# First norm and first four FFN tiles made block by block of rows, with the loads in that order

## The chip, the cores and the metric

The kernel runs on one core of a Trainium2 chip. The metric is device microseconds of one execution. Line numbers (L194) are those of the kernel file; in the changed kernel every helper stands one line lower (L195 for L194).

## The reference

The reference is two layers of a transformer block on 512 rows (256 of context, 256 of latent), each layer: a gated FFN half step, four parallel token mixers, another FFN half step. Only its first step matters here:

```python
def ada_mods(cond, w, b):
    m = jax.nn.silu(cond) @ w + b
    m = m.reshape(m.shape[:-1] + (N_MOD, D_MODEL))
    return [m[..., i, :][..., None, :] for i in range(N_MOD)]

def swiglu_half_step(x, g, shift, scale, gate, w1, w3, w2):
    h = modulate(rms_norm(x, g), shift, scale)      # h * (1 + scale) + shift
    return x + MACARON_W * gate * ((jax.nn.silu(h @ w1) * (h @ w3)) @ w2)
```

D_MODEL is 1024, D_FF is 2816 (22 tiles of 128), N_MOD is 9. The first half step needs modulations 0 (shift) and 1 (scale), one set for the context (`c_ctx`) and one for the latent rows (`c`).

## The kernel before

Data lie with features on the 128 partitions, in 8 blocks of 128 (`k`), and the 512 rows along the free axis: `X[128, 8, 512]`. Every large product is made in three matmuls per block, from a rounded high part and a residue of both operands (`hi`, `lo` of a weight, `hh`, `hl` of the normed rows): hi·hh, hi·hl, lo·hh. A weight tile (128 x 1024, 512 KB) is loaded to `wr` (3 buffers) by SyncE's queue (SP) and split in two halves (`parts`, `split`): ScalarE rounds the high part (`wh`, or `aa` and `ar` for the first tile), VectorE or POOL subtracts for the low part (`wl`). `LSEQ` and `EARLY` say which of the two does it, "V" or "P"; `EARLY[0]` is "PVPV".

The start of the program, up to the steady run of the first FFN, is what the change touches:

- `run` (L1863 and after) loads parameters, X in two halves, constants and a mask (`lvm`), makes the sums of squares (`sq_acc`), and runs `ada0`: 16 loads of 512 KB (two modulations, 8 blocks of the contraction), and for each block 4 matmuls of 512 columns with only 32 columns of weights (the conditions `cs`), all summed in one PSUM bank. `ada_finish` copies the result and transposes it. So the modulations of all 1024 features come out together, after the last load. After two of the 16 loads `rstd_a` sums the squares over the partitions (matmuls with one column) and takes the reciprocal root on VectorE.
- `norm` gives the normed rows in two column halves (rows 0 to 255, 256 to 511): `rstd_b` spreads the root over the partitions, then each block takes a product with x and the gain (VectorE, `nt`), a rounding with the shift added (ScalarE, `hh`) and a residue (VectorE, `hl`).
- `ffn` splits the weights of tiles f = 0 and 1 (w1 and w3 each: four products, which I call the first four FFN tiles), and `heads` makes the four products over the first half of the columns, then over the second. Then the loop over f takes w1 and w3 of a tile over all 512 columns, 24 matmuls each, with the activation behind, and steps the background work `ada` (the other modulations, on VectorE: scale and add, 128 x 1024) in between.

Matmuls of one engine run in the order in which a scheduler has put them when the kernel is built; `issue_after` and `high_priority` steer it, and a tile name with few buffers makes a later writer wait for its readers.

Of the kernel before, what the change touches and what calls it, by code (L numbers as in the profile page):

```python
# [8 lines left out]
F32 = mybir.dt.float32  # L9
# [4 lines left out]
ALU = mybir.AluOpType  # L14
# [11 lines left out]
def bc(ap, axis, n):  # L26
    a = ap.unsqueeze(axis)
    shp = list(a.shape)
    shp[axis] = n
    return a.broadcast_to(shp)  # L30


def constants():
# [93 lines left out]
class Ker:  # L127
# [1205 lines left out]
    def gemm(s, ps, hi, lo, xh, xl, n, first, last, m=128, mid=None):  # L1333

        for k in range(n):
            if k == n // 2 and mid:
                sec = s.sec
                mid()
                s.sec = sec
            st, sp = first and k == 0, last and k == n - 1  # L1340
            s.mm(ps, hi[k][:, 0:m], xh(k), start=st, stop=False)
            s.mm(ps, hi[k][:, 0:m], xl(k), start=False, stop=False)
            s.mm(ps, lo[k][:, 0:m], xh(k), start=False, stop=sp)
# [20 lines left out]
    def ada0(s, pool):  # L1364

        raws = {}
        cs = s.t(pool, "cs", [128, 8, 32])
        s.nc.gpsimd.memset(cs, 0.0)
        s.nc.vector.tensor_copy(cs[:, :, 0:2], s.cs)
        ps = s.psum("o")  # L1370
        for n in range(KC + 4):
            if n < KC:
                raws[n] = [s.ada_fetch(0, i, n, pool, 12) for i in range(2)]
            if n >= 4:
                kc = n - 4
                s.sec = "ada0"
                for j in range(4):
                    s.mm(ps[32 * j:32 * j + 32], cs[:, kc], raws[kc][j // 2][:, 512 * (j % 2):512 * (j % 2) + 512], start=(kc == 0), stop=(kc == KC - 1))
                yield
        v = s.ada_finish(0, 0, 2, ps)  # L1380
        ov = s.mod[0][:, 0:16].rearrange("p (j q) t -> p j q t", q=4)
        bv = s.p["adab"][:, 0, 0:16].rearrange("p (j q) -> p j q", q=4)
        s.tt(ov, v[:, :, :, 0:2], bc(bv, 3, 2), ALU.add)

    def ada(s, todo):

# [179 lines left out]
    def ffn(s, l, j, lat, bga, bgb, nxt):  # L1566

        nc = s.nc
        a = 256 if lat else 0
        hh, hl, part, todo = s.nh  # L1570
        gate = s.t(s.xp, "gate", [128, 8, 2], bufs=2)
        with s.tc.tile_pool(name=s.nm("fp"), bufs=1) as fp:
            gh, gl = (s.moved(fp, z, FF, 16) for z in ("gh", "gl"))
            with s.tc.tile_pool(name=s.nm("fa"), bufs=1) as fa:
                s.ar = (fa, 3, 2, hl[:, 7, 511:512].bitcast(F32))
                s.bg = [s.ada(bga)]
                def early(i, dram):
# [3 lines left out]
                ws = [early(i, s.I[n][l, j, 0]) for i, n in enumerate(("w1", "w3"))]  # L1581
                with s.tc.issue_after(s.lastq.ins) if lat else nullcontext():
                    ws += [s.piece(s.I[n][l, j, 1]) for n in ("w1", "w3")]
                hs4 = [s.psum("gm"[i % 2]) for i in range(4)]
                s.lseq = LSEQ["ffa"]
                s.heads(ws, hs4, (hh, hl), lat, todo or part(256 if lat else 0, 512 if lat else 256), part)
# [276 lines left out]
    def run(s, out):  # L1863
# [9 lines left out]
        with s.tc.tile_pool(name="st", bufs=1) as st:  # L1873
            for k in range(0, 8, 4):
                nc.sync.dma_start(s.X[:, k:k + 4], s.I["xT"][:, k:k + 4])
            nc.sync.dma_start(s.cst[:, 0:129], s.I["cst"][:, 0:129])
            lv = s.t(st, "lv", [128, 384])
            nc.sync.dma_start(lv, s.I["lvm"])
            nc.gpsimd.tensor_copy(s.mk.rearrange("p a b -> p (a b)"), lv)
            s.tt(s.i64, s.ident[:, 0:64], s.ident[:, 64:128], ALU.add, nc.gpsimd)  # L1880
            s.sec = "x"
            for d in range(7):
                s.sq_acc(d, 0, 512)
            for sp in s.parts2(False):
                s.sq_acc(7, *sp)
            s.bg = [s.ada0(st)]
            s.step(2)
            s.early = {sp[0]: s.rstd_a(*sp) for sp in s.parts2(False)}
            s.step(1000)
        s.late = [(s.cst[:, 129:], s.I["cst"][:, 129:CST_OFF["cos"][0]])]  # L1890
        nil = lambda p: []
        s.nh = *s.norm(0, 0), None
# [77 lines left out]
def pack_weights(inp):  # L1970
# [50 lines left out]
```

## Time and profile before

| | us |
|---|---|
| median of 3 runs (2442.76 to 2445.41) | 2444.49 |
| the profiled execution | 2443.27 |
| its span, first to last instruction | 2441.5 |
| TensorE busy | 2351.9 (96%) |
| VectorE busy | 1717.7 (70%) |
| ScalarE busy | 977.9 (40%) |
| POOL busy | 164.9 (7%) |
| read from HBM | 311.45 MB |

The profiled execution took 2443.27 us, of which 1.8 lie around its span. Busy shares are means over a program of many stages; what a change in the first 64 us is worth is read from those 64 us. In the profile an fp32 matmul stands as two records, and a matmul's duration is longer than its distance to the next one, because matmuls are pipelined. "x24" merges 24 instructions of a kind.

### The profile page before, as it was taken

The numbers are of one execution on the slowest core, as the hardware profiler recorded it, in microseconds if no ns is written. First come the engines' busy times: TensorE is split into PE (matmuls) and PEld (weight loads), VectorE is DVE, ScalarE is ACT, GpSimd is POOL, SyncE is SP. The second block draws the span as 40 slices with busy tenths as digits, with TensorE's granted clock in tenths as the row PEclk, the third lists the DMA queues.
The fourth block names the chain that finished last, engine by engine and source line by source line (L and its number), as shares of the span: only waits on it lengthen the run. The fifth ranks groups of instructions, "written<-read, shape, count | busy, mean of one in ns | idle before, by whom it ended". The sixth has DMA issues, their size and how long they took to land.

```text
span 2441.5 us, 41204 instructions
## 1 busy us (share of the span) xinstructions
PE 2351.9 (96%) x15690; PEld 1957.5 (80%) x15690; DVE 1717.7 (70%) x4146; ACT 977.9 (40%) x1900; POOL 164.9 (7%) x167
## 2 busy tenths in 40 slices
PE   7999999999999999999999999999999989898998
PEld 4887788867778788888788887878887868788998
DVE  4888797667865676688886787853367876786555
ACT  4333323344454443433332333332233654455554
POOL 1111100000000000011110011110000000000110
PEclk9999999999999999999999999999999999899999
DMA  6656444421212122366634455643343312234554
GB/s 266 206 198 212 151 138 156 152 84 57 78 61 70 53 79 70 131 205 207 207 96 134 142 174 189 208 138 93 98 132 116 105 57 92 80 120 158 184 181 136
DMA packets 116902, 330.34 MB, mean 135 GB/s; under 512 B 11872, under 2 KB 38624, under 8 KB 116320
## 3 DMA queue, kind: packets, MB, share of 16 engines
q1 hardware_dynamic: 116704, 327.71, 41.2%
q8 instruction: 123, 2.02, 0.3%
q14 instruction: 75, 0.61, 0.1%
HBM read 311.45 MB, written 16.22 MB: 134 GB/s over the span
## 4 chain that ended last, share of the span: by engine, by line
PE 85%; DVE 8%; ACT 3%; DMA 2%; issue 2%; POOL 0%; SPq 0%; DVEq 0%; ACTq 0%; POOLq 0%
PE ffa__g L194 17%; PE ffa__m L194 17%; PE ffb__g L194 15%; PE mrg__g L194 9%; PE win__g L194 8%; PE dn__m L194 3%; PE mrg__p L194 2%; PE out__g L194 2%; PE s__m L194 2%; PE hg__m L194 1%; PE at__m L194 1%; DMA s5ab<-tab__s5o 1%; DVE dn__it L212 1%; DVE dn__iw L212 1%; DMA ada__ar<-in_ada 1%
## 5 line engine op out<-in xcount | busy, mean ns | idle before, releaser
L209 ACT ACTIVATE ffa__wh<-ffa__wr 128x512 fp32r<-128x512 f32 x336 | 211.3, 631 | 421.5 <-PE ffa__m L194 151.4
L215 DVE SCALAR_TENSOR_TENSOR ada__aa<-ada__ar,x__cs,ada__aa 128x1024 f32<-128x1024 f32 x224 | 314.2, 1428 | 18.0 <-DMA ada__ar<-in_ada 17.4
L212 DVE TENSOR_TENSOR ffa__wl<-ffa__wr,ffa__wh 128x512 fp32r<-128x512 f32 x334 | 231.8, 702 | 125.4 <-ACT ffa__wh L209 124.2
L194 PE MATMUL ffa__g<-nrm__hh,ffa__wh 128*128 128x512 f32 (+1 forms) x696 | 250.1, 359 | 0.0
L194 PE MATMUL ffa__g<-nrm__hh,ffa__wl 128*128 128x512 f32 (+1 forms) x696 | 249.3, 358 | 0.0
L194 PE MATMUL ffa__g<-nrm__hl,ffa__wh 128*128 128x512 f32 (+1 forms) x696 | 248.6, 357 | 0.0
L194 PE MATMUL ffa__m<-nrm__hh,ffa__wh 128*128 128x512 f32 (+1 forms) x696 | 248.5, 357 | 0.0
L194 PE MATMUL ffa__m<-nrm__hl,ffa__wh 128*128 128x512 f32 (+1 forms) x696 | 248.3, 357 | 0.0
L194 PE MATMUL ffa__m<-nrm__hh,ffa__wl 128*128 128x512 f32 (+1 forms) x696 | 247.9, 356 | 0.0
L212 DVE TENSOR_TENSOR ffb__wl<-ffb__wr,ffb__wh 128x512 fp32r<-128x512 f32 x192 | 123.8, 647 | 144.2 <-ACT ffb__wh L209 143.2
L209 ACT ACTIVATE ffb__wh<-ffb__wr 128x512 fp32r<-128x512 f32 x192 | 113.9, 595 | 238.8 <-PE ffb__g L194 190.1
L194 PE MATMUL mrg__g<-nrm__hh,mrg__wh 128*128 128x256 f32 (+1 forms) x440 | 153.2, 348 | 3.8 <-ACT mrg__wh L209 1.9
L194 PEld LDWEIGHTS ffa__g<-nrm__hh,ffa__wh 128*128 128x128 f32 x696 | 132.3, 190 | 27.2 <-ACT ffa__wh L209 9.2
L194 PE MATMUL mrg__g<-nrm__hh,mrg__wl 128*128 128x256 f32 (+1 forms) x440 | 149.6, 340 | 2.9 <-DVE mrg__wl L212 2.9
L194 PEld LDWEIGHTS ffa__m<-nrm__hh,ffa__wh 128*128 128x128 f32 x696 | 131.7, 189 | 22.0 <-ACT ffa__wh L209 3.4
L194 PE MATMUL mrg__g<-nrm__hl,mrg__wh 128*128 128x256 f32 (+1 forms) x440 | 148.9, 338 | 0.0
L194 PEld LDWEIGHTS ffa__g<-nrm__hh,ffa__wl 128*128 128x128 f32 x696 | 132.0, 190 | 18.5
L194 PEld LDWEIGHTS ffa__g<-nrm__hl,ffa__wh 128*128 128x128 f32 x696 | 132.1, 190 | 18.3
L194 PEld LDWEIGHTS ffa__m<-nrm__hh,ffa__wl 128*128 128x128 f32 x696 | 131.6, 189 | 18.6
L194 PEld LDWEIGHTS ffa__m<-nrm__hl,ffa__wh 128*128 128x128 f32 x696 | 131.6, 189 | 18.4
L209 ACT ACTIVATE mrg__wh<-mrg__wr 128x512 fp32r<-128x512 f32 x128 | 79.6, 630 | 140.7 <-PE mrg__g L194 63.3
L194 PE MATMUL ffb__g<-nrm__gh,ffb__wh 128*128 128x256 f32 (+1 forms) x374 | 123.5, 330 | 0.0
(637 smaller groups left out, 5568.7 us busy)
## 6 DMA issues: line engine op xcount, KB each, us to landing
ffa__wr<-in_w SPq DMA_DIRECT2D x176, 512.0 KB, 3.9
ada__ar<-in_ada SPq DMA_DIRECT2D x144, 512.0 KB, 4.1
ffb__wr<-in_w SPq DMA_DIRECT2D x64, 512.0 KB, 3.5
mrg__wr<-in_wgt SPq DMA_DIRECT2D x64, 512.0 KB, 3.5
win__wr<-in_win SPq DMA_DIRECT2D x48, 512.0 KB, 3.6
ffb__wr<-in_w SPq DMA_DIRECT2D x32, 384.0 KB, 3.1
mrg__wr<-in_wbr SPq DMA_DIRECT2D x16, 512.0 KB, 3.5
out__wr<-in_wout SPq DMA_DIRECT2D x16, 512.0 KB, 3.9
```

The source lines that it names most:

```text
L194: s.last = s.nc.tensor.matmul(out=out, lhsT=lhsT, rhs=rhs, start=start, stop=stop, skip_group_check=True)
L209: s.lasta = s.nc.scalar.activation(out=out, in_=in_, func=f, **kw)
L212: (eng or s.nc.vector).tensor_tensor(out=out, in0=a, in1=b, op=op)
L215: s.nc.vector.scalar_tensor_tensor(out=out, in0=a, scalar=sc, in1=b, op0=op0, op1=op1)
```

## The change

`start0` takes the place of `ada0`, of the first `norm` and of the first `heads`. The weights of the first two modulations are packed anew (`in_ada0`): one piece of 1 MB for each block of 128 output features, holding the whole contraction for its shift and its scale. For each block there are 8 matmuls of 256 columns (`products`; contraction blocks 0 to 3 and 4 to 7 land in four column groups of the array), a copy by ScalarE, and two matmuls with the two columns of a new constant `sel4`, which add the four groups and turn the result (`block`; I call them the selection). Then the block's modulation, gain, product, rounding and residue follow for all 512 rows, and `gemm` gives this block's three matmuls of 512 columns to each of the four tiles, tiles 2 and 3 two blocks behind tiles 0 and 1. Loads are issued in the order of use. All low parts of the weights are made by VectorE. The mask's load goes behind all this, into a buffer of the norm. The raw pieces lie in the room of `gh` and `gl`, which are taken again afterwards. The background modulations and everything behind the first four tiles stay.

```diff
-EARLY = ("PVPV", "VVVV", "VVVV", "VVVV")
+EARLY = ("VVVV", "VVVV", "VVVV", "VVVV")
...
+    c["sel4"] = p[:, None] % 32 == np.arange(2)[None]
...
+    def start0(s, fp, early, ps4):
...
+        nc.sync.dma_start(s.X[:, 0:4], s.I["xT"][:, 0:4])
+        fetch(0)
+        nc.sync.dma_start(s.X[:, 4:8], s.I["xT"][:, 4:8])
...
+        for k in (1, 2):
+            fetch(k)
...
+        def products(k):
+            s.sec = "ada0"
+            ps = s.psum("p")
+            for kc in range(8):
+                j = kc % 4
+                s.mm(ps[32 * j:32 * j + 32, 0:256], cs[:, kc], raw[k][:, kc], start=(kc < 4), stop=(kc >= 4))
+            ev = room[0][:, 8192 + 256 * (k % 4):8448 + 256 * (k % 4)]
+            s.act(ev, ps[:, 0:256], AF.Copy)
+            return ev
+
+        def block(k, ev):
+
+            s.sec = "ada0"
+            for i in range(2):
+                s.mm(ms[:, 4 * k + 2 * i:4 * k + 2 * i + 2], ev[:, 128 * i:128 * i + 128], s.c["sel4"])
...
+            s.tt(mod, ms[:, 4 * k:4 * k + 4].rearrange("p (i t) -> p i t", i=2), bc(bias, 2, 2), ALU.add)
+            s.stt(gs[:, k], mod[:, 1], 1.0, s.p["ng"][:, 0, k:k + 1].broadcast_to([128, 2]), ALU.add, ALU.mult)
+            s.sec = "nrm00"
+            pair = s.t(s.xp, "nt", [128, 2, 256], bufs=2)
+            for z, (x, y, w) in enumerate(s.segs(0, 512)):
+                t, h, b = pair[:, z], hh[:, k, x:y], mod[:, 0, w:w + 1]
+                s.stt(t, s.X[:, k, x:y], gs[:, k, w:w + 1], r[:, x:y], ALU.mult, ALU.mult)
+                s.act(h, t, AF.Identity, bias=b)
+                s.stt(hl[:, k, x:y], t, b, h.bitcast(F32), ALU.add, ALU.subtract)
+
+        def gemm(t, k):
...
+            s.mm(ps, hi[k], hh[:, k], start=(k == 0), stop=False)
+            s.mm(ps, hi[k], hl[:, k], start=False, stop=False)
+            s.mm(ps, lo[k], hh[:, k], start=False, stop=(k == 7))
+        evs = {}
+        evs[0] = products(0)
+        with s.inorder():
+            evs[1] = products(1)
+        with s.inorder():
+            ys = [s.rstd_a(*sp) for sp in s.parts2(False)]
+        weights((0, 0), (0, 1))
+        fetch(3)
+        fetch(4)
...
+        for k in range(8):
+            if k < 7:
+                with s.inorder():
+                    block(k + 1, evs.pop(k + 1))
+            with s.inorder():
+                gemm(0, k)
+                gemm(1, k)
+            if k + 4 < 8:
+                with s.inorder():
+                    evs[k + 4] = products(k + 4)
+            with s.inorder():
+                if k >= 2:
+                    gemm(2, k - 2)
+                    gemm(3, k - 2)
...
+        lv = s.t(s.xp, "nt", [128, 512], bufs=2)[:, 0:384]
+        nc.sync.dma_start(lv, s.I["lvm"])
...
+    o["ada0"] = A["ada_w"][0].reshape(8, 128, 9, 8, 128)[:, :, 0:2].transpose(3, 1, 0, 2, 4).reshape(8, 128, 2048)
```

The printed order of TensorE shows the move. Before, from the last products (`x__o`, 4 matmuls for each contraction block) through the spread of the norm (`nrm__m`) and the transposes (`ada__p`) to the first FFN matmuls, of 256 columns (`ffa__g`, `ffa__m` are tiles of w1 and w3):

```order
L194 MATMUL x__o_128<-ada__ar_203,x__cs_125 32x512 x2
L194 MATMUL x__o_128<-ada__ar_205,x__cs_125 32x512 x2
L194 MATMUL nrm__m_290<-cst,x__rq_166 128x128 x2
L202 MATMUL ada__p_229<-cst,ada__rst_227 128x128 x4
L194 MATMUL ffa__g_286<-nrm__hh_238,ffa__aa_252 128x256
L194 MATMUL ffa__g_286<-nrm__hl_239,ffa__aa_252 128x256
```

Of the change, from products(2) to products(4) and selection(2): `ada__p` are a block's products, `nrm__o` its selection, `nrm__m` the two halves of the spread.

```order
L195 MATMUL ada__p_214<-ffa__gh_102,ffa__gl_103 32x256 x8
L195 MATMUL nrm__m_224<-cst,ada__rq_167 128x128 x2
L195 MATMUL nrm__m_228<-cst,ada__rq_184 128x128 x2
L195 MATMUL nrm__o_141<-cst,ffa__gh_102 128x2 x2
L195 MATMUL ada__p_253<-ffa__gl_103 32x256 x8
L195 MATMUL nrm__o_141<-cst,ffa__gh_102 128x2 x2
L195 MATMUL ffa__g_98<-nrm__hh_138,ffa__aa_198 128x512
L195 MATMUL ffa__g_98<-nrm__hl_139,ffa__aa_198 128x512
L195 MATMUL ffa__g_98<-nrm__hh_138,ffa__aa_199 128x512
L195 MATMUL ffa__m_99<-nrm__hh_138,ffa__ar_206 128x512
L195 MATMUL ffa__m_99<-nrm__hl_139,ffa__ar_206 128x512
L195 MATMUL ffa__m_99<-nrm__hh_138,ffa__ar_207 128x512
```

The FFN matmuls now stand behind four of the eight blocks' products instead of behind all of them, and the other four stand among them.

On VectorE, in the change, from the modulation of block 0 (`x__mod`) to its last residue (`nrm__hl`); `aa` and `ar` are the low parts of the first tile's w1 and w3:

```order
L213 TENSOR_TENSOR x__mod_2_77<-nrm__o_141,prm 128x2x2
L213 TENSOR_TENSOR ffa__aa_199<-ffa__wr_196,ffa__aa_198 128x512 x2
L216 SCALAR_TENSOR_TENSOR nrm__gs_137<-x__mod_2_77,prm 128x2
L216 SCALAR_TENSOR_TENSOR nrm__nt_246<-x__X_76,nrm__gs_137,nrm__rst_140 128x256
L213 TENSOR_TENSOR ffa__ar_207<-ffa__wr_204,ffa__ar_206 128x512 x2
L216 SCALAR_TENSOR_TENSOR nrm__hl_139<-nrm__nt_246,x__mod_2_77,nrm__hh_138 128x256
L216 SCALAR_TENSOR_TENSOR nrm__nt_246<-x__X_76,nrm__gs_137,nrm__rst_140 128x256
L216 SCALAR_TENSOR_TENSOR nrm__hl_139<-nrm__nt_246,x__mod_2_77,nrm__hh_138 128x256
```

Four splits of half a tile stand inside the chain of block 0; two of them were POOL's.

## Rows read from the trace of the kernel before

**Rows 1.** The page: busy time of each engine with its share of the span, and the shares of the chain that ended last.

```profile
PE 2351.9 (96%) x15690; PEld 1957.5 (80%) x15690; DVE 1717.7 (70%) x4146; ACT 977.9 (40%) x1900; POOL 164.9 (7%) x167
...
PE 85%; DVE 8%; ACT 3%; DMA 2%; issue 2%; POOL 0%; SPq 0%; DVEq 0%; ACTq 0%; POOLq 0%
```

**Rows 2.** The chain that ended last, in order of time, in the first 140 us: start in us, length in us, what (x16 is a count of instructions).

```profile
3.31 7.18 DMA ada__ar<-in_ada
...
13.70 3.50 PE x__m L194 x16
...
19.51 9.70 DMA ada__ar<-in_ada
...
32.20 1.83 DVE nrm__nt L215 x3
...
35.83 1.89 DVE nrm__hl L215 x2
37.72 1.69 DVE ffa__ar L212
...
39.45 0.80 PE ffa__m L194 x2
...
63.90 5.47 PE ffa__g L194 x24
69.36 5.44 PE ffa__m L194 x24
```

**Rows 3.** Stretches: from:to and length in us, busy time of PE, PEld, DVE, ACT and POOL with their instructions, granted TensorE clock, DMA share, GB/s.

```profile
20.00:25.00 5.00, 4.94 (x28) 1.08 (x20) 0.00 (x0) 0.00 (x0) 0.00 (x0) 1.00 1.03 421
...
36.00:37.00 1.00, 0.64 (x3) 0.64 (x4) 1.00 (x2) 0.84 (x2) 1.00 (x1) 0.52 0.45 86
...
42.00:43.00 1.00, 1.00 (x7) 1.00 (x7) 1.00 (x3) 0.97 (x3) 0.00 (x0) 0.56 1.05 397
```

**Rows 4.** Instructions in order of time in the old head and norm, merged: start us, length us (of all that are merged), engine, line, operation, what it writes and reads.

```profile
31.70 0.19 DVE L212 TENSOR_TENSOR x__mod<-ada__p,prm 128x32 f32<-128x32 f32 x1 [12.34 <-PE ada__p L202]
...
32.60 3.31 DVE L215 SCALAR_TENSOR_TENSOR nrm__nt<-x__X,x__gs,nrm__rst 128x256 f32<-128x256 f32 x3
32.74 2.89 POOL L212 TENSOR_TENSOR ffa__aa<-ffa__wr,ffa__aa 128x512 fp32r<-128x512 f32 x2 [22.07 <-ACT ffa__aa L209]
...
43.09 1.28 DVE L212 TENSOR_TENSOR ffa__wl<-ffa__wr,ffa__wh 128x512 fp32r<-128x512 f32 x2
...
49.10 1.32 ACT L209 ACTIVATE nrm__hh<-nrm__nt,x__mod 128x256 fp32r<-128x256 f32 x3 [0.55 <-DVE nrm__nt L215]
...
52.15 1.27 DVE L215 SCALAR_TENSOR_TENSOR nrm__hl<-nrm__nt,x__mod,nrm__hh 128x256 fp32r<-128x256 f32 x3
```

**Rows 5.** The issue of X's two loads by SP (start and length in us), and, from the view of the tile X, the time from an issue to its landing.

```profile
1.19 0.89 SPq L1875 DMA_DIRECT2D x__X<-in_xT  x2
...
DMA to landing us min/median/max: 4.9/5.9/7.0
```

**Rows 6.** The old products by records, from the view of their tile in two stretches (duration in ns, shortest/median/longest; first and last start in us); then, in order of time, the last of the reciprocal root on VectorE and one half of the spread on TensorE.

```profile
L194 PE MATMUL x__o<-ada__ar,x__cs x8: 1061/1061/1061, 20.5 to 21.4; 128*32 128x512 f32 x8
L194 PE MATMUL x__o<-ada__ar,x__cs x8: 592/592/593, 22.8 to 23.6; 128*32 128x512 f32 x8
...
18.89 0.48 DVE L215 SCALAR_TENSOR_TENSOR x__rq<-x__rq 128x2 f32<-128x2 f32 x4
...
30.23 0.71 PE L194 MATMUL nrm__m<-cst,x__rq 128*128 128x128 f32 x4
```

**Rows 7.** TensorE in order of time at two places where small fp32 matmuls stand in a dense stream of 512-column ones: 8 records with 32 columns of weights, and 8 records (4 matmuls) with two moving columns.

```profile
107.06 0.39 PE L194 MATMUL ffa__m<-nrm__hh,ffa__wl 128*128 128x512 f32 x1
107.38 1.06 PE L194 MATMUL ada__o<-ada__aa,cst 128*32 128x512 f32 x8
...
108.70 0.39 PE L194 MATMUL ffa__g<-nrm__hl,ffa__wh 128*128 128x512 f32 x1
...
585.78 0.39 PE L194 MATMUL win__g<-nrm__hl,win__wh 128*128 128x512 f32 x1
586.03 1.05 PE L194 MATMUL dn__m<-cst,dn__nt 128*128 128x2 f32 x8
586.94 0.48 PE L194 MATMUL win__g<-nrm__hh,win__wl 128*128 128x512 f32 x1
587.25 0.39 PE L194 MATMUL win__g<-nrm__hh,win__wh 128*128 128x512 f32 x1
```

**Rows 8.** Stretches of 1 us, with the columns of rows 3, around a short gap late in the program.

```profile
1949.00:1950.00 1.00, 0.21 (x1) 0.00 (x0) 1.00 (x3) 0.98 (x3) 0.00 (x0) 1.00 0.09 12
...
1951.00:1952.00 1.00, 0.93 (x4) 0.93 (x5) 1.00 (x1) 0.95 (x4) 0.00 (x0) 0.50 0.68 279
...
1954.00:1955.00 1.00, 1.00 (x10) 1.00 (x9) 1.00 (x2) 0.85 (x2) 0.00 (x0) 0.83 0.00 0
```

**Rows 9.** VectorE behind the head, in order of time, and one stretch of 10 us with the columns of rows 3.

```profile
59.08 2.50 DVE L221 TENSOR_SCALAR ada__aa<-ada__ar,x__cs 128x1024 f32<-128x1024 f32 x2
...
72.73 2.47 DVE L215 SCALAR_TENSOR_TENSOR ada__aa<-ada__ar,x__cs,ada__aa 128x1024 f32<-128x1024 f32 x2
...
96.67 0.69 DVE L212 TENSOR_TENSOR ffa__nt<-ffa__nt,ffa__m 128x512 f32<-128x512 f32 x1 [1.35 <-PE ffa__m L194]
...
70.00:80.00 10.00, 10.00 (x46) 8.29 (x45) 10.00 (x12) 2.78 (x5) 1.66 (x1) 1.00 0.66 209
```

More of the change, by code (lines that the diff above doesn't have):

```diff
@@ L1362, in ada_finish, with fetch, weights @@
         return pt.rearrange("p (q j x) -> p j q x", q=4, x=32)
[L1364 to L1383, printed above, removed]
+    def start0(s, fp, early, ps4):
+        nc = s.nc
+        sec = s.sec
+        HEAD = ((0, 0), (0, 1), (1, 0), (1, 1))
+        room = [s.t(fp, z, [128, 512 * FF + 64], bufs=1) for z in ("gh", "gl")]
+        raw = [z[:, 2048 * i:2048 * i + 2048].rearrange("p (a b) -> p a b", b=256) for i in range(4) for z in room]
+        def fetch(k):
+            s.sec = "ada0"
+            nc.sync.dma_start(raw[k].rearrange("p a b -> p (a b)"), s.I["ada0"][k])
+        ws = {}
+        def weights(*n):
+            for f, i in n:
+                s.sec = sec
+                ws[f, i] = early(f, i)
+        nc.sync.dma_start(s.X[:, 0:4], s.I["xT"][:, 0:4])
+        fetch(0)
+        nc.sync.dma_start(s.X[:, 4:8], s.I["xT"][:, 4:8])
+        n1 = CST_OFF["bones"][0]
+        nc.sync.dma_start(s.cst[:, 0:n1], s.I["cst"][:, 0:n1])
+        for k in (1, 2):
+            fetch(k)
+        cs = room[1][:, 8192:8448].rearrange("p (k m) -> p k m", m=32)
+        nc.gpsimd.memset(cs, 0.0)
+        nc.vector.tensor_copy(cs[:, :, 0:2], s.cs)
+        s.tt(s.i64, s.ident[:, 0:64], s.ident[:, 64:128], ALU.add, nc.gpsimd)
+        s.sec = "x"
+        for d in range(7):
+            s.sq_acc(d, 0, 512)
+        for sp in s.parts2(False):
+            s.sq_acc(7, *sp)
+        s.sec = "nrm00"
+        gs = s.t(s.xp, "gs", [128, 8, 2], bufs=1)
+        hh, hl = (s.moved(s.xp, z, 8, 48) for z in ("hh", "hl"))
+        r = s.t(s.xp, "rst", [128, 512], bufs=1)
+        ms = s.psum("o")
+        def products(k):
[8 more added lines that the diff above has]
+        def block(k, ev):
+            s.sec = "ada0"
+            for i in range(2):
+                s.mm(ms[:, 4 * k + 2 * i:4 * k + 2 * i + 2], ev[:, 128 * i:128 * i + 128], s.c["sel4"])
+            mod = s.mod[0][:, 0:16].rearrange("p (i k) t -> p i k t", i=2)[:, :, k]
+            bias = s.p["adab"][:, 0, 0:16].rearrange("p (i k) -> p i k", i=2)[:, :, k]
+            s.tt(mod, ms[:, 4 * k:4 * k + 4].rearrange("p (i t) -> p i t", i=2), bc(bias, 2, 2), ALU.add)
+            s.stt(gs[:, k], mod[:, 1], 1.0, s.p["ng"][:, 0, k:k + 1].broadcast_to([128, 2]), ALU.add, ALU.mult)
+            s.sec = "nrm00"
+            pair = s.t(s.xp, "nt", [128, 2, 256], bufs=2)
[5 more added lines that the diff above has]
+        def gemm(t, k):
+            s.sec = sec
+            hi, lo = ws[HEAD[t]]
+            ps = ps4[t]
+            s.mm(ps, hi[k], hh[:, k], start=(k == 0), stop=False)
[11 more added lines that the diff above has]
+        with s.inorder():
+            evs[2] = products(2)
+        for sp, y in zip(s.parts2(False), ys):
+            with s.inorder():
+                s.sec = "nrm00"
+                s.rstd_b(y, r, *sp)
+        weights((1, 0))
+        with s.inorder():
+            block(0, evs.pop(0))
+        with s.inorder():
+            evs[3] = products(3)
+        fetch(5)
+        weights((1, 1))
+        fetch(6)
+        fetch(7)
+        for k in range(8):
+            if k < 7:
+                with s.inorder():
+                    block(k + 1, evs.pop(k + 1))
+            with s.inorder():
+                gemm(0, k)
+                gemm(1, k)
+            if k + 4 < 8:
+                with s.inorder():
+                    evs[k + 4] = products(k + 4)
+            with s.inorder():
+                if k >= 2:
+                    gemm(2, k - 2)
+                    gemm(3, k - 2)
+        for t in (2, 3):
+            with s.inorder():
+                gemm(t, 6)
+                gemm(t, 7)
+        lv = s.t(s.xp, "nt", [128, 512], bufs=2)[:, 0:384]
+        nc.sync.dma_start(lv, s.I["lvm"])
+        nc.gpsimd.tensor_copy(s.mk.rearrange("p a b -> p (a b)"), lv)
+        s.sec = sec
+        return hh, hl
@@ L1569, in ffn, with early @@
         a = 256 if lat else 0
-        hh, hl, part, todo = s.nh
+        hh, hl, part, todo = s.nh or (None,) * 4
         gate = s.t(s.xp, "gate", [128, 8, 2], bufs=2)
         with s.tc.tile_pool(name=s.nm("fp"), bufs=1) as fp:
-            gh, gl = (s.moved(fp, z, FF, 16) for z in ("gh", "gl"))
             with s.tc.tile_pool(name=s.nm("fa"), bufs=1) as fa:
-                s.ar = (fa, 3, 2, hl[:, 7, 511:512].bitcast(F32))
-                s.bg = [s.ada(bga)]
-                def early(i, dram):
+                def early(f, i):
+                    dram = s.I["w3" if i else "w1"][l, j, f]
+                    if f:
+                        return s.piece(dram)
                     return s.parts(s.fetch(dram), tiles=[s.t(fa, "ar" if i else "aa", [128, 8, 128], F32R, bufs=3) for _ in range(2)])
@@ L1580, in ffn @@
                 s.lseq = EARLY[2 * l + j]
[L1581 to L1584, printed above, removed]
+                if not s.nh:
+                    hs4 = [s.psum("gm"[i % 2]) for i in range(4)]
+                    hh, hl = s.start0(fp, early, hs4)
+                else:
+                    ws = [early(0, i) for i in range(2)]
+                    with s.tc.issue_after(s.lastq.ins) if lat else nullcontext():
+                        ws += [early(1, i) for i in range(2)]
+                    hs4 = [s.psum("gm"[i % 2]) for i in range(4)]
+                    s.lseq = LSEQ["ffa"]
+                    s.heads(ws, hs4, (hh, hl), lat, todo or part(256 if lat else 0, 512 if lat else 256), part)
                 s.lseq = LSEQ["ffa"]
-                s.heads(ws, hs4, (hh, hl), lat, todo or part(256 if lat else 0, 512 if lat else 256), part)
+                gh, gl = (s.moved(fp, z, FF, 16) for z in ("gh", "gl"))
+                s.ar = (fa, 3, 2, hl[:, 7, 511:512].bitcast(F32))
+                s.bg = [s.ada(bga)]
                 while s.late:
@@ L1872, in run @@
         s.act(s.cs, s.p["cc"], AF.Silu)
[L1873 to L1890, printed above, removed]
+        n1 = CST_OFF["bones"][0]
+        s.late = [(s.cst[:, n1:], s.I["cst"][:, n1:CST_OFF["cos"][0]])]
+        s.early = {}
         nil = lambda p: []
-        s.nh = *s.norm(0, 0), None
+        s.nh = None
         s.ffn(0, 0, False, [(0, i) for i in range(2, 8)], lambda p: [s.s5_tables(p, 0, s.W[0])], (0, 1))
```

## The prediction

> **What bounds the kernel now.** I read the page first: TensorE is busy 96% of the span and carries 85% of the chain that ended last [rows 1]. So time is won only where TensorE waits, runs at the low clock, or does work that can go. Then I read the chain in order of time [rows 2]. The reader should see a start-up with little FFN work in it: loads until 10.49 (3.31 + 7.18), TensorE on small work, loads again until 29.21 (19.51 + 9.70), and then pieces on VectorE (32.20 to 39.41). Only from 39.45 on are the pieces FFN matmuls one behind another. At 63.90 the first matmul of tile f = 2 starts. I call everything before it the head; from there a tile takes 5.44 us and nothing but TensorE stands on the chain. The third view is the stretches [rows 3]: 421 GB/s between 20 and 25 us (loads at their limit), and, once TensorE has stood still for those pieces on VectorE, its clock granted at 0.52 between 36 and 37 and still at 0.56 between 42 and 43 (0.50 is 1.2 GHz, 1.00 is 2.4 GHz).
>
> From the printed orders, the instructions of all engines behind the first tiles of this FFN stand as before. So the time should move by what the 63.90 moves, provided nothing behind it starts to wait. The sum is made against the profiled execution, 2443.27 us; the median of the three runs, 2444.49, lies 1.2 above it.
>
> **When the loads land.** X's first half lands at 6.1 (issued at 1.19, 4.9 later [rows 5]). Sixteen modulation pieces of 0.5 MB land from 10.49 to 29.21 [rows 2], 1.25 us each, so 2.5 us per MB. In the new order the blocks of ada0 land at 8.6 (0), 13.8 (1, behind X's second half and the constants), 16.3 (2), then two weight pieces until 18.8, and 21.3, 23.8, 27.6, 31.4 and 33.9 (3 to 7). The last byte comes when it came before, give or take 1 us; what changes is what can be done with the first of them.
>
> **When the first FFN matmul starts.** TensorE's order is products(0), products(1), the 16 column sums of the norm, products(2), the spread of the norm, selection(0), products(3), selection(1), first FFN matmul.
> - Products: 64 matmuls of 256 columns in place of 32 of 512, so the same columns. A record took 1061 ns until 21.4 and 592 ns from 22.8 [rows 6], although the view of stretches shows 1.00 there; I go by the records and price early work at the low clock. Eight records of 512 columns in a stream at full clock cost 1.19 us: 108.70 - 107.06 less two matmuls of 0.227 [rows 7]. A block has the same columns: 1.2 us at full clock, 1.8 at the low one. Products(1) run 13.8 to 15.6.
> - The sums take 3.5 us [rows 2], until 19.1. The reciprocal root on VectorE ends 2.1 us after the sums (19.37 against 17.20 [rows 6, 2]), at 21.2. Products(2) lie beside it. The spread, two halves of 0.6 us (0.71 for one with its tail [rows 6]), begins as the first root is out and ends at 22.1.
> - Selection: two matmuls with 2 columns in place of the transposes. Four such matmuls in a stream cost 1.02 us (587.25 - 585.78 less two of 0.227 [rows 7]), so 0.5 for a block at full clock, 0.9 at the low one: 23.0.
> - The Trainium skill, "TensorE: Matmul & The Clock Gate", section "Wait — 56ns, not 53.3ns?", puts the floor between starts of tiny matmuls at about 25 ns. By that figure a selection would cost 0.1 us, and the head would end some 2.5 us earlier than in my sum. The row shows about 0.25 us per fp32 matmul with new 128-column weights, and the row decides.
> - VectorE then has, in order: modulation 0.2, two low-half splits of w1 1.3, the gain 0.2, one product with x 0.42, two splits of w3 1.3, a residue, a product and ScalarE's rounding (0.42, 0.42, 0.46) [rows 4]. That is 4.7 us, 4.8 with hops: **27.8**.
>
> The four splits that POOL did cost VectorE 2.6 us here, twice 1.28 [rows 4], but free it of POOL's company: three products took 3.31 us while POOL split, and 1.27 for three residues without it [rows 4].
>
> **What TensorE then has to do.** 96 matmuls of 512 columns at 0.227 (5.44 / 24 [rows 2]) are 21.8 us; before it was 192 of 256 columns. What used to lie under the loads now lies in this stream: products(4) to (7), 4 x 1.2 = 4.8, and selections (2) to (7), 6 x 0.5 = 3.0. Sum 29.6, so 57.4 at full clock.
>
> The clock: TensorE idles some 2 us before 27.8. At 1950 an idle stretch of under 2 us was enough for 0.50, and dense work brought the high clock back some 3 us later; in the old head it took over 6 us, with gaps in them [rows 8, 3]. I take the low clock until 33, 5.2 us at half speed: 2.6 lost. With 0.2 of waits the head ends at **60.2**, 3.7 us before 63.90. Bounds: 55.0 if the clock is full all the time, 65.0 if it is low until 45.
>
> Does VectorE keep up? A block costs it 0.2 + 0.2 + 4 x 0.42 and hops, 2.2 us; TensorE needs at least 3.2 for a block (four tiles at 0.68 and a selection). Yes, with about 1 us in hand. ScalarE copies a block's products (256 columns) and rounds twice as many, about 3 x 0.46: less still. Loads: the last block lands at 33.9, TensorE reaches it at about 42.
>
> **What is queued behind the new waits.** The mask load (192 KB) now stands on SP's queue behind the weight loads of f = 2 and 3, and in front of the background modulations; it waits for a buffer of the last norm blocks. The first background piece waited for the last residue before too. Its data come 3.5 to 4 us behind that residue, so VectorE's scaling starts at about 58.4 (59.08 before [rows 9]). From there VectorE has its usual mixture, splits of 0.64 [rows 4] between steps of 1.2 us [rows 9]. The split for the second tile of f = 2 comes at 61.5 and is needed at 66, the one for f = 3 at 69 and needed at 71.4. VectorE has 2 us in hand, and at 96.67 it waited for TensorE before. So I cost this at nothing; without that margin it would be 1 to 2 us. POOL's mask conversion now has to end before the second gate activation, at 59, since that takes over the mask's buffer; its load is issued at about 55, which leaves it room. Tables and constants are wanted much later: nothing.
>
> **Sum.** 2443.27 - 3.7 = 2439.6, or 2440.8 counted from the median. I say **2440.0**, 0.18% under the median. A measurement of this kernel can tell about 0.2% from no change, 4.9 us: faster means under 2439.6.
>
> **Rivals.**
> - *The clock is up early.* Products(2), the spread, selection(0) and products(3) follow each other closely from 19 to 25.6, and the high clock outlives the 2 us before 27.8. Then the head ends at 55 to 57 and the time is 2434.5 to 2436.5. For it: the records went to 592 ns at 22 before, in a stream of products [rows 6]. Against: those were dense from 17.1 on, and the drop at 1950 came after a gap as short [rows 8]. Chance 0.17.
> - *The clock stays low, and the kernel gets slower.* The one mechanism that ends on the other side: TensorE's work is now cut into pieces between waits for loads and for VectorE, and the low clock lasts as long as the products do, to 45. The head then ends at 65.0, 1.1 us later than before: 2444.4 to 2445.6. It decides from a clock that comes back later than 43. Low through the whole head, it would be 80.9 and 2460. For it: the low clock for over 6 us in the old head [rows 3]. Against: from 27.8 on the sum has no gap above 0.5 us. The Trainium skill speaks for this rival: the same page, section "HAM oscillation — how this bites in real kernels", advises doing all k steps of one output together, since work cut up by waits for loads keeps the engine cold; this change does the opposite. Here the loads are ahead of TensorE from block 4 on, so I hold it to be the smaller case. Chance 0.15.
> - *The gain is swallowed behind the head.* VectorE is some 6 us less ahead of TensorE than before; if its 2 us of margin are not there, TensorE waits for splits at f = 2 to 4 and the time is 2441.5 to 2443.5. For it: VectorE was busy all of 70 to 80 before [rows 9]. Against: the margins worked out above. Chance 0.13.
>
> **How the numbers follow.** My case has 0.55 and its own range is 2437.5 to 2442.0 (runs of this kernel lie up to 1.7 us from their median, the start is known to 1 us, and the clock comes back between 31 and 35). Some two fifths of it lie below 2439.6, which with the early clock makes 0.40 faster; 0.04 slower by over 0.2% from the worst of the low clock; 0.56 within. The range, 2435.0 to 2445.0, leaves out the best of the first rival and the worst of the second.
>
> **What would show it.** First FFN matmul at 27 to 29; last one at 59 to 61; the granted clock 0.50 at 28 to 31 and 1.00 from 35; no TensorE gap over 0.5 us behind 28; products within the stream at 1.2 us a block; VectorE waiting for TensorE between blocks. Wrong would be a first matmul behind 30, VectorE ending each block later than TensorE's stream, a low clock behind 40, or waits for splits between 61 and 80.

## The result, and the profile after

The changed kernel takes 2459.80 us (median of 13 runs, 2452.93 to 2465.00), the kernel before in the same session 2445.52 (13 runs, 2439.52 to 2454.33). The ratio is 1.005, 95% interval 1.004 to 1.0061: by the ratio some 12 us slower (the medians lie 14.3 apart), where 4 us faster was forecast. The profiled execution of the changed kernel took 2460.72 us with a span of 2458.9, against 2443.27 and 2441.5 before. Its page, for [rows 1]:

```profile
PE 2372.1 (96%) x15686; PEld 1958.5 (80%) x15686; DVE 1717.1 (70%) x4164; ACT 981.1 (40%) x1907; POOL 154.3 (6%) x163
...
PE 87%; DVE 6%; ACT 2%; DMA 2%; issue 1%; POOL 0%; DVEq 0%; SPq 0%; ACTq 0%; POOLq 0%
```

TensorE has four records fewer and is busy 20.2 us longer. So the loss is not a wait: matmuls take longer. The chain that ended last, in order of time, for [rows 2] (start us, length us, what):

```profile
26.45 1.29 DVE ffa__ar L213 x2
...
28.56 0.52 ACT nrm__hh L210
29.08 0.04 issue
29.12 1.74 PE ffa__g L195 x3
30.86 1.28 PE ffa__m L195 x3
32.15 1.87 PE ada__p L195 x16
34.01 0.95 PE nrm__o L195 x4
...
37.73 1.37 PE ada__p L195 x16
39.09 0.54 PE nrm__o L195 x4
39.63 0.80 PE ffa__g L195 x3
40.43 0.69 PE ffa__m L195 x3
41.13 1.00 PE ada__p L195 x16
...
62.04 1.39 PE ffa__m L195 x6
63.43 5.58 PE ffa__g L195 x24
69.01 5.57 PE ffa__m L195 x24
```

Two things are to be seen. The head ends at 63.43, where it ended at 63.90 before: the gain of 3.7 us shrank to 0.5. And behind it a tile of 24 matmuls takes 5.58 us instead of 5.44: 232.5 ns between the starts of two matmuls, which I call the pitch, and 226.7 before. No wait stands between them. The head by TensorE's records (start, length, in brackets the idle time before and what ended it):

```profile
21.74 2.08 PE L195 MATMUL nrm__m<-cst,ada__rq 128*128 128x128 f32 x8 [0.23 <-DVE ada__rq L216]
...
26.25 1.01 PE L195 MATMUL nrm__o<-cst,ffa__gh 128*128 128x2 f32 x4
29.12 0.80 PE L195 MATMUL ffa__g<-nrm__hh,ffa__aa 128*128 128x512 f32 x1 [1.86 <-ACT nrm__hh L210]
...
31.09 0.63 PE L195 MATMUL ffa__m<-nrm__hl,ffa__ar 128*128 128x512 f32 x1
...
40.50 0.40 PE L195 MATMUL ffa__m<-nrm__hl,ffa__ar 128*128 128x512 f32 x1
```

A matmul takes 0.63 us at 31.09 and 0.40 at 40.50, 0.43 and 0.23 from start to start: the low and the high clock. The change comes at about 38. The view of stretches does not show it, unlike in [rows 3], and here the records decide: in each trace the list of granted clocks begins with its first rise (38.46 us here, 22.39 in the kernel before), and a stretch ahead of that entry is shown as 1.00. So the clock had not been high at all before 38.46.

```profile
37.00:38.00 1.00, 1.00 (x6) 0.20 (x9) 0.82 (x3) 0.58 (x2) 0.00 (x0) 1.00 0.43 104
```

Where the 17.4 us between the spans lie, from the start of the first matmul of each stage in the two traces (us):

| stage | before | after | difference |
|---|---|---|---|
| head, to the first matmul of f = 2 | 63.9 | 63.4 | -0.5 |
| first FFN, first half, from there | 227.0 | 232.3 | +5.3 |
| second FFN, first half | 251.9 | 257.3 | +5.4 |
| third FFN, first half | 252.2 | 259.9 | +7.7 |
| fourth FFN, first half (256 columns) | 128.9 | 128.1 | -0.8 |
| both mixer stages | 963.9 | 964.2 | +0.3 |
| all the rest | | | 0.0 |

The three first halves with 512 columns hold all of it, 20 tiles of f with two products each: 120 x 0.14 = 16.8 us. The third lost 2 us more than its tiles account for, and the traces show where: from its start to the first tile of 512 columns it took 28.54 us and not 26.26, since the low clock lasted until 1427.7 there and before only until 1411.6. The same eight matmuls, before and after:

```profile
1412.25 0.79 PE nrm__m L194 x8
...
1423.46 1.50 PE nrm__m L195 x8
```

This is not the tiles' loss: after_pad128B, below, has tiles as slow and took 26.2 us for that stretch. By pairs of neighbouring starts, every matmul that reads hh or hl went from 227 to 232.6 ns there; those that read gh, gl, mh or ml stayed at 226 to 228. In the mixers the 512-column matmuls on hh and hl lengthened too (228.5 to 232.6 ns), but TensorE had idle time there (12 us in the first mixer stage), and the stages' time hardly moved. The instructions behind the head are in the same order. What did change is where hh and hl lie: "gs", "hh", "hl" and "rst" are now allocated in another order. In the built programs hh's first byte in a partition is 78656 before and 76736 after, a multiple of 256 plus 64 and plus 192; wh and wl lie at plus 64 in both, aa and ar at a multiple of 256.

### The profile page after: what moved, and what is told of

Read it like the earlier page. It is cut to its first block, busy times and chain, and to the rows that moved or that the text cites. A ratio compares the mean times of both kernels' runs of the same rounds, so it can differ in the third digit from the quotient of the medians.

```text
span 2458.9 us, 41207 instructions
## 1 busy us (share of the span) xinstructions
PE 2372.1 (96%) x15686; PEld 1958.5 (80%) x15686; DVE 1717.1 (70%) x4164; ACT 981.1 (40%) x1907; POOL 154.3 (6%) x163
## 4 chain that ended last, share of the span: by engine, by line
PE 87%; DVE 6%; ACT 2%; DMA 2%; issue 1%; POOL 0%; DVEq 0%; SPq 0%; ACTq 0%; POOLq 0%
PE ffa__g L195 18%; PE ffa__m L195 18%; PE ffb__g L195 15%; PE mrg__g L195 10%; PE win__g L195 9%; PE dn__m L195 3%; PE mrg__p L195 2%; PE out__g L195 2%; PE s__m L195 2%; PE hg__m L195 1%; PE at__m L195 1%; DMA s5ab<-tab__s5o 1%; DVE dn__it L213 1%; PE nrm__m L195 1%; DVE tab__s5big L213 1%
## 5 line engine op out<-in xcount | busy, mean ns | idle before, releaser
L195 PE MATMUL ffb__g<-nrm__gh,ffb__wh 128*128 128x512 f32 (+1 forms) x572 | 195.8, 342 | 0.0
L195 PE MATMUL ffb__g<-nrm__gh,ffb__wl 128*128 128x512 f32 (+1 forms) x572 | 195.0, 341 | 0.0
L195 PE MATMUL ffb__g<-nrm__gl,ffb__wh 128*128 128x512 f32 (+1 forms) x572 | 194.7, 340 | 0.0
```

Source lines behind the costliest of these rows:

```text
L195: s.last = s.nc.tensor.matmul(out=out, lhsT=lhsT, rhs=rhs, start=start, stop=stop, skip_group_check=True)
```

## The experiments

Runs with one time each are read from their traces, since single runs of one kernel spread over some 12 us. In the fences that follow, rows are pieces of the chain: a tile of 24 matmuls of 512 columns, then one of 24 of 256 columns in the last FFN (5.44 and 2.88 before, 5.58 and 2.85 after).

**hh and hl back at plus 64, in the changed kernel.**

```diff
-        hh, hl = (s.moved(s.xp, z, 8, 48) for z in ("hh", "hl"))
+        hh, hl = (s.moved(s.xp, z, 8, 16) for z in ("hh", "hl"))
```

> The changed kernel with one thing altered: hh and hl, the two halves of the norm's result, begin 16 columns into their buffers and not 48. Their first byte in a partition is then again a multiple of 256 plus 64, as in the kernel before (78656 for hh), where the changed kernel has plus 192 (76736), since its buffers were allocated in another order. Theory A (the place of the moving operand sets the pitch): 512-column matmuls that read hh or hl go back from 232.6 to 227 ns; TensorE's busy time falls from 2372 to about 2352 us; the time falls by some 15 to 20 us to 2440 to 2445, and what is left against the kernel before is the change's own worth, which the head of the profile puts at a gain of 0.5 to 1 us. Theory B (something else that the change moved slows the matmuls: the place of the other buffers, the loads, a lower clock): 232.6 ns stay, and the time stays at 2459 to 2460.

```profile
63.42 5.44 PE ffa__g L195 x24
...
2263.72 2.88 PE ffa__g L195 x24
```

2445.17 us (12 runs), 0.9996 of the kernel before (0.9986 to 1.0005); TensorE busy 2355.2 us. Theory A held: 32 columns less of offset, and the whole loss is gone. Without it the change is worth some 1 us, not told from none.

**The same offset in the kernel before**, where it makes plus 192: the same line, 48 to 16.

> The kernel before with hh and hl 16 columns into their buffers and not 48: their first byte is then a multiple of 256 plus 192, as in the changed kernel; nothing else differs, not one instruction moves. Theory A: 512-column matmuls on hh and hl go from 227 to 232 to 233 ns, some 4000 of them, so the time rises by 15 to 22 us to 2460 to 2467. Theory B: nothing changes, 2444 to 2446.

```profile
64.55 5.58 PE ffa__g L194 x24
...
2268.62 2.85 PE ffa__g L194 x24
```

2460.05 us (4 runs), 1.006 (1.0047 to 1.0073); busy 2370.2 us. The old kernel, with nothing of the change in it, loses the same time, so the head plays no part in it.

**hh alone moved back.**

```diff
-        hh, hl = (s.moved(s.xp, z, 8, 48) for z in ("hh", "hl"))
+        hh, hl = (s.moved(s.xp, z, 8, o) for z, o in (("hh", 16), ("hl", 48)))
```

> The changed kernel with hh alone 16 columns into its buffer (plus 64 over a multiple of 256) and hl left at 48 (plus 192). Theory A, with each matmul paying for its own moving operand: matmuls that read hh run at 227 ns and those that read hl at 232.6, side by side in one run; two thirds of the loss come back, so about 2446 to 2448. If instead the distance between hh and hl counts, both kinds change alike. Theory B: 232.6 for both, 2459 to 2460.

```profile
62.24 5.60 PE ffa__g L195 x24
...
2264.29 2.83 PE ffa__m L195 x24
```

2452.56 us (one run). The expectation of theory A fell: no matmul came back. The pitch is 233.9 ns for hh with wh, 232.5 for hl with wh and 231.0 for hh with wl. A matmul does not pay for its own operand alone; one operand in three out of place slows all three.

**All buffers moved by 128 bytes**, the weights' too.

```diff
+        s.pad = s.cp.tile([128, 32], F32, name="pad")
+        nc.gpsimd.memset(s.pad, 0.0)
```

> The changed kernel with one unused buffer of 128 bytes in a partition among the constants, so that all buffers behind it move by 128 bytes: hh and hl to a multiple of 256 plus 64, gh and gl (the gate's halves, read by the FFN's second half) to plus 192, and the weights' halves wh and wl from plus 64 to plus 192. If the place of the moving operand alone counts: hh and hl 227 ns, gh and gl 232 to 233; about 2445 to 2449. If its place against the weights' counts: hh and hl stay at 232.6, since weights and operand move together, and gh and gl stay at 227.5: 2459 to 2460.

```profile
63.21 5.58 PE ffa__g L197 x24
...
2265.50 2.85 PE ffa__g L197 x24
```

2456.95 us (one run). hh now has the remainder 64 that was fast before, and it is slow; gh and gl have 192 and run at 227 ns. So it is not the byte itself that counts but the place against the other buffers, which moved with it; of these a matmul reads only its weights.

**Both edits:** the 128 bytes of the last run and offset 16 of the first.

> The changed kernel with the unused 128 bytes of after_pad128B and hh, hl at 16 columns: hh begins at 76736, the very byte at which it stands in the slow changed kernel, hl at 93376, likewise, but the weights' halves now stand at a multiple of 256 plus 192, like both. Theory A2 (what counts is the remainder by 256 against the weights' halves): 227 ns for 512 columns and 120.0 for 256, and 2441 to 2447. If the byte itself counted, or hh's distance to any buffer that did not move: 232.6 and 118.6, 2452 to 2462.

```profile
61.70 5.44 PE ffa__g L197 x24
...
2264.36 2.88 PE ffa__g L197 x24
```

2440.22 us (one run). hh and hl stand on the very bytes at which they are slow in the changed kernel, and with weights of the same remainder they are fast. Theory A2 holds.

**64 bytes apart:** the first run's line with 32 in place of 48 (above the weights' remainder), then with 0 (below it).

> The changed kernel with hh and hl 32 columns into their buffers: 76672 and 93312, a multiple of 256 plus 128, where the weights' halves wh and wl stand at plus 64. The runs so far: all of weights, hh and hl at the same remainder by 256 give 227 ns for a 512-column matmul and 120.0 for one of 256 columns; 128 bytes apart, 232.6 and 118.6, whether operand or weights were moved. Theory A2 (the remainder by 256 against the weights' counts, and only the same one is fast for 512 columns): 64 bytes apart is slow too, 230 to 233 ns, and 256 columns run at some 115 to 117, as they did in the old head on weights that stood 64 bytes off. Theory A3 (the remainder by 128 counts, and 64 bytes apart is worst): above 233. Rival A4: only a distance of 128 hurts, and this is back at 227.

```profile
63.65 5.49 PE ffa__g L195 x24
...
2262.26 2.83 PE ffa__m L195 x24
```

> The changed kernel with hh and hl at the start of their buffers: 76544 and 93184, multiples of 256, 64 bytes below the weights' remainder, where the 32-column offset stands 64 above. Theory A2: as with 32 columns, 230 to 233 ns for 512 columns and 115 to 117 for 256. Rival A4: 227. If the sign counts, this and the run with 32 columns differ.

```profile
62.17 5.60 PE ffa__g L195 x24
...
2272.81 2.83 PE ffa__g L195 x24
```

2450.53 and 2463.42 us (one run each). 64 above costs little (5.49 / 24 = 228.8 ns a matmul, under the 230 expected), 64 below as much as 128 (233.3): the sign counts, which A2 had not said. With 256 columns all of these are faster than the same remainder: 2.83 and 2.85 against 2.88. The range for 256 columns, 115 to 117 ns, was too low: 118.

That it is the weights' place, and not that of some other buffer, shows within one run, where the same hh meets two kinds of weights. In after_off0 it has the remainder of aa and ar, and 256 columns take 120 ns on those and 118 on wh and wl; in after_off16 it has the remainder of wh and wl, and they take 118 on aa and ar and 120 on wh and wl (medians between neighbouring starts at the high clock).

**Zeros in the gaps of the head**, to see what the low clock costs there: matmuls that nobody reads, on top of after_off16.

```diff
+            for _ in range(n):
+                s.mm(ps, hot[:, 0:128], hot)
...
-        evs[0] = products(0)
+        warm(20)
+        with s.inorder():
+            evs[0] = products(0)
+        with s.inorder():
+            warm(14)
...
+            if k == 0:
+                with s.inorder():
+                    warm(12)
```

> The changed kernel with hh and hl at 16 columns (so without the loss on the matmuls), and with matmuls of zeros that nobody reads in the places where TensorE waits in the head: 20 of 512 columns in bf16 ahead of the first products, 14 ahead of the second, 12 ahead of the first FFN matmul. They write a buffer of the products and change no result. The head of after_off16: first FFN matmul at 29.37, 0.43 us a matmul until 37.9, head ends at 63.42. Theory C (the low clock is what ate the head's gain): the records are at the high clock from 20 at the latest, the first FFN matmul comes at 26 to 28, the head ends at 56 to 59, and the time falls by 4.5 to 7 us to 2438 to 2441. Rival D (the head waits for VectorE and for the loads of the last blocks, and a faster TensorE only waits longer): it ends above 61 and the time moves by less than 2.5 us. A third case: the zeros don't raise the clock, 0.43 us stay and nothing moves, or the head is later by the dummies' own time.

```profile
9.03 1.07 PE L195 MATMUL ada__p<-ffa__gh,ffa__gl 128*32 128x256 f32 x16 [1.23 <-DMA ffa__gh<-in_ada]
...
14.16 1.07 PE L195 MATMUL ada__p<-ffa__gl 128*32 128x256 f32 x16 [1.14 <-ACT x__nt L210]
...
17.04 1.07 PE L195 MATMUL ada__p<-ffa__gh,ffa__gl 128*32 128x256 f32 x16
19.20 2.08 PE L195 MATMUL nrm__m<-cst,ada__rq 128*128 128x128 f32 x8 [1.09 <-DVE ada__rq L216]
...
25.39 4.32 PE L195 MATMUL nrm__p<-ffa__gl 128*128 128x512 bf16 x10 [0.22 <-issue]
29.31 0.63 PE L195 MATMUL ffa__g<-nrm__hh,ffa__aa 128*128 128x512 f32 x1
...
30.24 0.39 PE L195 MATMUL ffa__m<-nrm__hh,ffa__ar 128*128 128x512 f32 x1
```

2442.56 us (11 runs), 0.9992 (0.9983 to 1.0001). The first FFN matmul comes no earlier, since the zeros stood in its way at the low clock; but from it to the end of the head (59.30 in the chain) it is 29.99 us, where after_off16 needs 34.05 (29.37 to 63.42). So the low clock cost the stream 4.1 us, and that part of theory C holds. The rest of it does not: the low clock came back at 19.2, behind 1.09 us of standing still (1.07 us for 16 records at 17.04, 2.08 for 8 at 19.20), and lasted until 29.4; the head ends at 59.30, where 56 to 59 was expected; and the time is 2.6 us under after_off16 of an earlier session, where 4.5 to 7 was expected, and not told from the kernel before.

**POOL makes its four splits again**, on top of after_off16: run once, and then timed.

```diff
-EARLY = ("VVVV", "VVVV", "VVVV", "VVVV")
+EARLY = ("PVPV", "VVVV", "VVVV", "VVVV")
```

> after_off16 with one part of the change undone: POOL again makes the low halves of the w1 pieces of f = 0 and f = 1, the four splits that the change gave to VectorE. What is asked is the first FFN matmul (29.37 in after_off16) and the end of the head (63.42). If VectorE's splits hold the first matmul: it comes up to 1.2 us earlier, at 28.2 to 28.8, and the head ends at 62 to 63. If POOL's company slows VectorE's products again, as in the old head (three took 3.31 us): 29 to 31, and the head ends at 63.4 or later. The time itself moves by less than a single run can tell.

> The kernel of after_off16_pool once more, now timed beside the kernel before. In its first trace the first FFN matmul came at 27.03 and not 29.37, without a gap behind the second selection, the records went over to the high clock at about 31 and not 38, and the head ended at 58.80 and not 63.42, 5.1 us before that of the kernel before (63.90). Theory E (the splits that the change moved from POOL to VectorE made the gap that kept the clock low, and nothing behind the head takes the gain back): 4 to 6 us less than the kernel before, a ratio of 0.9975 to 0.9985. Rival (the first trace was a lucky one, or the gain is given back behind the head): the head ends above 62, or the ratio is 0.9990 or more.

The single run:

```profile
26.16 1.01 PE L195 MATMUL nrm__o<-cst,ffa__gh 128*128 128x2 f32 x4
27.03 0.77 PE L195 MATMUL ffa__g<-nrm__hh,ffa__aa 128*128 128x512 f32 x1
...
32.71 0.39 PE L195 MATMUL ffa__g<-nrm__hh,ffa__aa 128*128 128x512 f32 x1
```

The timed run:

```profile
24.85 0.61 PE L195 MATMUL nrm__o<-cst,ffa__gh 128*128 128x2 f32 x4
26.57 0.67 PE L195 MATMUL ffa__g<-nrm__hh,ffa__aa 128*128 128x512 f32 x1 [1.11 <-ACT nrm__hh L210]
28.02 0.79 PE L195 MATMUL ffa__g<-nrm__hl,ffa__aa 128*128 128x512 f32 x1 [0.78 <-DVE nrm__hl L216]
28.61 0.63 PE L195 MATMUL ffa__g<-nrm__hh,ffa__aa 128*128 128x512 f32 x1
...
26.00:27.00 1.00, 0.43 (x1) 0.19 (x1) 1.00 (x2) 0.78 (x3) 0.00 (x0) 0.87 1.03 414
```

The first FFN matmul comes at 27.03 and 26.57, not 29.37: more than either case allowed. In the single run no gap stands before it, and the records reach the high clock at about 31; the head ends at 58.96. In the timed run the high clock was there at 24.85; it fell at 26.7, behind a gap of 1.11 us (the last row: 0.87 granted from 26 to 27) and ahead of the second gap of 0.78, stayed low until about 37, and the head ends at 61.72. 2444.30 us (12 runs), 0.9991 (0.9981 to 1.0001): the part of theory E on the start holds; the part on the time, 4 to 6 us, does not, since the clock's return is not the same in each run, and 2 us are less than the timing tells.

**Towards a better kernel.** best_warm_lat32 is after_off16_warm with 6 more zeros behind products(2) and, in the last FFN, hh, hl, gh and gl at offset 32. best_pool_warm_lat32 has POOL's splits as well, 8 zeros ahead of products(3), and none ahead of the first FFN matmul.

```diff
             evs[2] = products(2)
+        with s.inorder():
+            warm(6)
...
-        hh, hl = (s.moved(s.xp, z, 8, 16) for z in ("hh", "hl"))
+        hh, hl = (s.moved(s.xp, z, 8, 32 if (l, j) == (1, 2) else 16) for z in ("hh", "hl"))
...
-                gh, gl = (s.moved(fp, z, FF, 16) for z in ("gh", "gl"))
+                gh, gl = (s.moved(fp, z, FF, 32 if lat else 16) for z in ("gh", "gl"))
```

> after_off16_warm with two more edits. First, 6 more matmuls of zeros behind the third products, where TensorE stood still for 1.09 us and the low clock came back until 29.3. Second, in the last FFN, where all matmuls have 256 columns, hh and hl and gh and gl at 32 columns, 64 bytes above the weights' remainder, where 256 columns took 117.6 ns and not 120.0. Expected if the low clock is what the head still pays: records at the high clock from 9 to the end, first FFN matmul at 25.5 to 27.5, head ends at 55.5 to 57.5 (59.6 in after_off16_warm). In the last FFN 117.5 to 118 ns, some 1500 matmuls, 3 to 4 us less. Together 6 to 8 us below after_off16_warm: 2434 to 2437, 0.9955 to 0.9975 of the kernel before. Rival (what the head gains is given back behind it, since VectorE then is less ahead): the head ends as early, but waits of 2 us or more stand between 60 and 100, and the ratio is 0.998 or above.

> best_warm_lat32 with POOL's splits as in the kernel before, without the 12 matmuls of zeros ahead of the first FFN matmul (they ran at the low clock, 4.66 us, and held it at 29.85 though hh and hl were there at 24.8), and with 8 in the place where TensorE stood still for 2.04 us ahead of the products that wait for block 3. Expected: records at the high clock from 9 on, products(3) at 22.8 to 23.0 in 1.07 us, first FFN matmul at 24.4 to 26.5, head ends at 54.5 to 56.5 (59.62 in best_warm_lat32), the time 3 to 5 us below it: a ratio to the kernel before of 0.992 to 0.995. Rival: the last blocks' loads (to about 34) or VectorE now hold TensorE in the stream, with gaps of over 1 us between 26 and 40, and the head ends at 57 to 59.

best_pool_warm_lat32:

```profile
22.03 1.89 PE L195 MATMUL nrm__p<-ffa__gl 128*128 128x512 bf16 x8
23.85 1.07 PE L195 MATMUL ada__p<-ffa__gl 128*32 128x256 f32 x16
...
25.75 0.50 PE L195 MATMUL ffa__g<-nrm__hh,ffa__aa 128*128 128x512 f32 x1 [0.29 <-ACT nrm__hh L210]
...
33.47 0.51 PE L195 MATMUL ffa__g<-nrm__hl,ffa__aa 128*128 128x512 f32 x1 [0.78 <-DVE nrm__hl L216]
```

```profile
57.03 5.44 PE ffa__g L195 x24
...
2264.69 2.83 PE ffa__g L195 x24
```

The first took 2436.60 us (6 runs), 0.9946 (0.9928 to 0.9963), though its head ended only at 59.78: its 12 zeros ran at the low clock and held the first FFN matmul at 29.85. The second took 2438.02 (12 runs), 0.997 (0.996 to 0.9979), with a head that ends at 57.03, half a microsecond later than expected, with one wait of 0.78 on VectorE in it and the low clock from 16.9 to 20.3. Both beat the kernel before in their sessions and lie over 20 us under the changed kernel; which is the faster the runs do not tell, so the 3 to 5 us expected between them were not found. The last FFN's 256 columns are worth 0.05 us a tile in both, 3.0 and 2.2 us over its first half against after_off16_warm.

## Why the prediction was wrong

**"Nothing behind it starts to wait", so the time moves by what the head moves: this step failed.** It was true of the waits and false as a bound. I compared the order of the instructions and not the places of their operands. A change of allocation made each 512-column matmul on hh and hl 5.8 ns longer, 16.8 us in 120 tiles. Offset 16 takes it away, and the same offset puts it into the kernel before. No rival named it, so the range could not hold the time. The rival on slower than before was right in sign for another reason.

**The head: 60.2 forecast, 63.43 measured.** With the tiles at their old pitch it ends at 63.42 (after_off16), so the 3.2 us too little are the head's own:
- *Start, 27.8.* It was 29.12, and 29.37 in after_off16. The loads, the sums and VectorE's 4.7 us (28.56 is ScalarE's rounding) came as summed, some 0.4 late. The spread came at 21.74 and took 2.08 us; I had it end at 22.1. At the high clock it takes 1.05 (the record of best_pool_warm_lat32 at 20.78), so this too was the low clock.
- *Clock, 2.6 lost until 33.* It stayed low until about 38 and cost 4.1 (34.05 against 29.99), 0.45 us for each of the 9.1 us from 29.4 to 38.5; my sum took 0.5. So the price was about right and the length too short. Here the mechanism of the second rival was right and its size between the two cases: the clock came back later than in my sum, and earlier than 43, where I put the turning point. The Trainium skill, "TensorE: Matmul & The Clock Gate", section "HAM oscillation — how this bites in real kernels", had spoken for that rival. The trace agrees with it further than I did: no record before 38 us ran at the high clock.
- *VectorE takes POOL's splits, costed as even.* It was not even. With POOL's splits back the first FFN matmul came 2.3 us earlier in the single run, at the same low clock and with no gap before it; in the timed run 2.8 us earlier, in part by a high clock from 23.3 to 26.7, and with a gap of 1.11. The chain before 29.12 runs through a split (26.45), so most of the 1.86 us in which TensorE stood still there came from the splits on VectorE, as far as one run can tell.
- *Stream, 29.6 at the high clock.* 29.99 in after_off16_warm: right. Products cost 1.00 us a block (1.2 forecast), a selection 0.34 (0.5 forecast), and the first matmul behind each some 0.1 more. The Trainium skill, "TensorE: Matmul & The Clock Gate", section "Wait — 56ns, not 53.3ns?", had led to an estimate of 0.1 for a selection; the 0.34 measured speaks against that price here.

**"VectorE keeps up", and no gain swallowed behind the head: right.** From 63.43 on a tile follows a tile without a wait, and where the head got shorter (59.30, 57.03) the next tiles still took 5.44.

**Open.** Why the operands' places against each other matter was not tried: no run shows where the reads meet. Nor is the remainder the whole rule: with hl alone out of place, hh on wh took 233.9 ns with the same remainder (after_hh16_hl48), and in the head of after_off0 some 30 matmuls of 512 columns on aa and ar took 231 with it. Why the low clock lasted longer at the start of the third FFN is not shown either.

## What to carry to other kernels

A comparison of instruction orders does not show where buffers lie. When a change allocates in another order, compare the addresses of the operands of the inner matmuls as well, here by their remainder against the weights'; and when TensorE is busy longer with no more instructions, divide a tile's time by its matmuls before looking for a wait. At the start of a kernel, price small TensorE work at the low clock until a record shows the high one, and move work off the engine that feeds the first dense matmuls, since a gap before them can cost more than its own length (with the 1.86 us gone, the head ended 4.5 us earlier in the single run; 1.7 in the timed run, with 1.11 left).

## What the runs showed of the hardware that was not expected

- The pitch of 512-column matmuls on fp32r data depends on the remainder by 256 of the moving operand's first byte against the weights': the same 226.7 ns, 64 above 228.8, 128 apart 232.5, 64 below 233.3, when hh and hl are moved together. The two lie 65 times 256 bytes apart (76736 and 93376) and behave alike, so no remainder by more than 256 is needed. With the same remainder nearly all pitches are 226 or 227 ns; 128 apart they spread from 228 to 241. The Trainium skill, "SBUF — State Buffer", section "SBUF: two separate sides", has TensorE never wait for another engine at that memory; the runs do not speak against it, since what they show is a cost from the places of one engine's own two operands.
- With 256 columns it is the other way round: 120.0 ns for the same remainder, 117.8 to 118.7 for the others, in the FFNs on wh and wl.
- The length of one gap does not tell whether the clock falls. It fell behind 1.09 us of standing still (after_off16_warm at 19.2) and behind 1.11 (after_off16_pool_timed at 26.7). It stayed high behind 1.23 and 1.14 us (after_off16_warm at 9.03 and 14.16) and 0.78 (best_pool_warm_lat32 at 33.47), and in best_pool_warm_lat32 it fell at 16.9 with no gap of 0.1 us before it (0.94 granted from 16 to 17, 0.50 from 17 to 18).
- A granted clock of 1.00 at the start of a trace can mean that there is no entry yet: the list begins with the first rise, from 5.5 us (after_off16_warm) to 38.9 (after_off32).
